# More dense blocks between shorter lists in the up stage of a two-layer encoder, with VectorE's order written out around the lists

## The chip, the core and the metric

The kernel is one program on one core of a Trainium2 chip. The core has five engines that run side by side and wait for each other by semaphores: TensorE (PE in the profile; PEld is its weight load), VectorE (DVE), ScalarE (ACT), GpSimd (POOL) and SyncE (SP). SP issues plain DMA transfers, POOL issues the indirect ones, whose rows are picked by a table of numbers. The metric is the time of one launch on the device in microseconds, as the median of some runs; smaller is better. A profile is taken of one more execution, and its span is a little shorter than that execution's time.

## The reference

Two layers over 256 frames of width 1024: first a latent attention, then a sparse attention, each followed by a channel mixer that picks experts by product keys. The mixer is what matters here:

```python
def _peer(x, w_q, sub_keys, w_down, w_up):
    ...
    best, pos = lax.top_k(cand, PEER_TOPK)
    expert = jnp.take_along_axis(cand_idx, pos, axis=-1)
    gate = jax.nn.softmax(best, axis=-1)
    ...
    def per_block(args):
        x_blk, e_blk, g_blk = args
        u = w_down[e_blk]
        a = jnp.einsum('td,ted->te', x_blk, u).astype(jnp.float32)
        hg = (jax.nn.gelu(a, approximate=False) * g_blk).astype(w_up.dtype)
        return jnp.einsum('te,ted->td', hg, w_up[e_blk]).astype(x_blk.dtype)
```

Each frame picks 8 x 16 = 128 of 16384 experts. For each it needs one row of `w_down` and one of `w_up`, both 1024 wide. All is float32.

## The kernel before

*Numbers.* Each float32 operand is cut in two float16 halves, a high one (`hi`, on ScalarE, L137) and what is left (`lo`, on VectorE, L146). A product is three matmuls on PE: hi with hi, hi with lo, lo with hi. The same holds for the second operand, cut into `xh` and `xl`. Every `lo` and `xl` also sums its entries into a column, from which the program judges at its end whether the halves and the lists were good enough; if not, the whole trunk runs once more in full float32.

*The mixer.* The 16384 experts stand as 128 blocks of 128 rows. The **down stage** takes every block against all 256 frames (`d`, 24 matmuls of 256 columns a block), applies the gelu and multiplies by the gates, which `place` spreads out from one-hot products (`G`). The result `A` (128 rows x 128 blocks x 256 frames) stays on the chip in `arena`. Beside `G` the product `seen` notes, for each half of the frames, which block's expert in a row is used by anybody.

The **up stage** sums `A` times `w_up` into four banks `y`: 12 matmuls of 512 columns for a block that both halves of the frames use, 6 for a block that only one half uses (`rows`). The first `HEAD` = 16 blocks are dense: their rows of `w_up` come by a plain DMA on SP (L192) and their `A` is taken from `arena`. For the other 112 blocks the program doesn't take all. In each of the 128 rows it makes three lists of the block numbers that are used: by both halves (`JB` = 40 places), by the first half only and by the second half only (`JO` = 24 places each). What doesn't fit goes into a common tail that is spread over all rows (`TB` = 12 places of 128 entries; a row may give up to `ROWTAIL` = 32). That makes 40 + 12 listed blocks of both halves and 48 of one. Each listed block is put together by POOL: one indirect DMA for its 128 rows of `w_up` (L190, tile `raw`) and one for its 128 rows of `A` (L1537 for both halves, L1543 for one, tiles `V` and `U`). For the second, `A` was copied to memory before (`abuf`, by `store`, L1454, in pieces of `CHUNKED` = 8 blocks and one half). Blocks are taken in groups of two or three that share one pair of slots in `xh` and `xl`.

*The lists* are made by `lists`, a generator (L1358 onward) that `list_on` moves forward step by step, partly beside the last down blocks, partly beside the dense head. It picks the eight largest numbers at a time (L1376, L1377), counts the tail, sums the counts over the rows with one small matmul (`base`, L1396), builds one-hot tiles (`wide`, `sent`, `to`) and sends the tail's entries to their rows with 32 small matmuls (`moved`, L1431). At its end stand `up_at` and `act_at`, the numbers that POOL's indirect DMAs read.

*What sets the order.* A scheduler orders each engine's instructions, except where the code links them: `pe`, `dve` and `act` put an instruction behind the one that the same chain issued last. In this kernel PE's matmuls of the two stages are linked, the lists' own are not. SP's transfers (plain rows of `w_up`, pieces of `abuf`) are one queue in order, and so are POOL's.

*The stream.* `Stream.get` hands out the next block of weights. It keeps six `raw` buffers and six pairs of `hi` and `lo`; it splits three blocks ahead and loads up to five more.

Of the kernel before, what the change touches and what calls it, by code (L numbers as in the profile page):

```python
# [10 lines left out]
F32 = mybir.dt.float32  # L11
F32R = mybir.dt.float32r
F16 = mybir.dt.float16
# [55 lines left out]
HEAD = 16  # L69
JB, JO, TB, ROWTAIL = 40, 24, 12, 32  # L70
# [3 lines left out]
CHUNKED = 8  # L74


def _up_order():
# [34 lines left out]
    return groups, items  # L112


GROUPS, ITEMS = _up_order()

# [32 lines left out]
class Stream:  # L149
# [16 lines left out]
    def listed(self, table, rows, order, unit, kind):  # L166
        for c in order:
            self.rows[len(self.blocks)] = table, rows[:, c : c + 1]
            self.blocks.append((None, D, unit))
            self.kind.append(kind)  # L170
# [129 lines left out]
def tile_trunk(ctx: ExitStack, tc: tile.TileContext, ins, out: bass.AP, short, shared):  # L300
# [56 lines left out]
    if short:  # L357
        abuf = dram.tile([(NKEYS + 1 - HEAD) * P, T], F32, tag="abuf", name="abuf")
# [8 lines left out]
        nc.vector.memset(weight16[:, :HEAD], 0.0)  # L367
        zero = arena[:, 30720 - T : 30720]
        nc.vector.memset(zero, 0.0)
        nc.sync.dma_start(abuf[(NKEYS - HEAD) * P :, :], zero)  # L370
# [764 lines left out]
    def peer(li):  # L1135
# [222 lines left out]
        def lists():  # L1358
# [7 lines left out]
            nc.vector.tensor_scalar(two, seen[:, : 2 * P].rearrange("p (t b) -> p t b", b=P), 0.0, None, op0=ALU.is_gt)  # L1366
            nc.vector.tensor_tensor(key[:, 0, :], two[:, 0, :], two[:, 1, :], op=ALU.mult)
            yield
            nc.vector.tensor_tensor(key[:, 1, :], two[:, 0, :], two[:, 1, :], op=ALU.is_gt)
            nc.vector.tensor_tensor(key[:, 2, :], two[:, 1, :], two[:, 0, :], op=ALU.is_gt)  # L1370
            nc.vector.tensor_tensor(key[:, 0:3, :], key[:, 0:3, :], weight16[:, None, :].to_broadcast([P, 3, P]),
                                    op=ALU.mult)
            yield

            def take(o, k):
                nc.vector.max(o, k)  # L1376
                nc.vector.match_replace(k, o, k, 0.0)  # L1377
# [6 lines left out]
            nc.vector.tensor_tensor(over, key[:, 0, :], key[:, 1, :], op=ALU.add)  # L1384
            nc.vector.tensor_tensor(over, over, key[:, 2, :], op=ALU.add)
# [4 lines left out]
            nc.vector.max(m8, over)  # L1390
            nc.vector.tensor_scalar(valid, more, 0.0, None, op0=ALU.is_gt)
            nc.vector.tensor_reduce(count[:, 0:1], valid, axis=AX.X, op=ALU.add)
            n16 = small.tile([P, 1], F16, tag="n16", name="n16", bufs=1)
            nc.vector.tensor_copy(n16, count[:, 0:1])
            p = ps("base")
            nc.tensor.matmul(p[:, 0:1], below16, n16, start=True, stop=True)  # L1396
            vals = small.tile([P, ROWTAIL, 2], F16, tag="vals", name="vals", bufs=1)
            nc.vector.tensor_copy(vals[:, :, 0], more)
            nc.vector.tensor_scalar(vals[:, :, 1], valid, row, None, op0=ALU.mult)
            yield  # L1400
            nc.vector.tensor_copy(count[:, 1:2], p[:, 0:1])
            rank, block = got[:, 3, 2 * ROWTAIL : 3 * ROWTAIL], got[:, 3, 3 * ROWTAIL :]
            nc.vector.tensor_scalar(rank, iota16[:, :ROWTAIL], count[:, 1:2], None, op0=ALU.add)
            nc.vector.tensor_scalar(block, rank, 1.0 / P, -(P - 1) / (2.0 * P), op0=ALU.mult, op1=ALU.add)
            nc.vector.tensor_scalar(block, block, MAGIC, None, op0=ALU.add)
            nc.vector.tensor_scalar(block, block, -MAGIC, None, op0=ALU.add)
            at16 = small.tile([P, 2, ROWTAIL], F16, tag="at16", name="at16", bufs=1)
            nc.vector.scalar_tensor_tensor(at16[:, 0, :], block, -float(P), rank, op0=ALU.mult, op1=ALU.add)
# [137 lines left out]
        def cut_group(g):  # L1546
            if g >= len(GROUPS):
                return
# [203 lines left out]
```

## Time and profile before

| what | us |
|---|---|
| median of three runs | 1775.59 (1774.29 to 1784.7) |
| the profiled execution, in all | 1780.97 |
| its span | 1778.7 |
| up stage of layer 0, first to last `y` matmul | 549.1 to 866.5 |
| up stage of layer 1 | 1450.4 to 1760.7 |
| POOL busy from 560 to 850, with 198 indirect DMAs | 228.5 |

How to read it: the page gives each engine's busy time and, in 40 slices, the tenths in which it was busy. A row of the timeline gives the start, how long, the engine, the line, the operation with its tiles (output, arrow, inputs) and in brackets how long the engine sat idle before, and for whom. A row of the windows gives, for a stretch, each engine's busy time with its number of instructions, then the clock that PE was granted (1.00 is full speed), the DMA engines' share and GB/s. A matmul of 512 columns is listed with 0.38 us, of which a part overlaps the next; its pace is read from start to start.

### The profile page before, as it was taken

What the parts mean: (1) busy time and instruction counts of PE and PEld (TensorE: products, weight loads), DVE (VectorE), ACT (ScalarE), POOL (GpSimd) and SP (SyncE); (2) the same over time, 40 slices, a digit from 0 to 9 for tenths busy, and PEclk for the clock granted to TensorE, in tenths of its full rate; (3) what the DMA queues carried; (4) which work ended last, traced back from release to release, by engine and by line L of the source; (5) the groups of instructions that cost most, each with busy time, mean ns of one, the idle gap of its engine ahead of it and who ended that gap; (6) DMA issues with size and microseconds to landing.
All of it is one profiled execution on the core that took longest, in us unless ns stands there. A gap on an engine that the chain in (4) does not pass through costs nothing.

```text
span 1778.7 us, 32888 instructions
## 1 busy us (share of the span) xinstructions
PE 1604.0 (90%) x12209; PEld 1152.1 (65%) x12209; DVE 1341.3 (75%) x3210; ACT 1060.5 (60%) x1846; POOL 636.5 (36%) x530
## 2 busy tenths in 40 slices
PE   9999999999988977877899999998999979788775
PEld 7688888899974433332478698887999944333232
DVE  8689999789997454554788799997899986445445
ACT  7666656788864444444577666666888735344343
POOL 2011343000003777777222112540000017777773
PEclk9999999899998989999999999998999989999997
DMA  9455656348578666666765455564466597666664
GB/s 343 152 171 183 197 199 218 126 159 272 184 214 293 212 222 204 221 210 218 268 230 199 169 184 201 196 209 149 160 210 237 193 325 234 210 212 226 214 198 156
DMA packets 156476, 372.44 MB, mean 209 GB/s; under 512 B 14096, under 2 KB 72592, under 8 KB 156304
## 3 DMA queue, kind: packets, MB, share of 16 engines
q1 hardware_dynamic: 119152, 244.91, 41.1%
q0 software_dynamic: 36864, 124.81, 21.8%
q8 instruction: 97, 1.59, 0.4%
q14 instruction: 75, 0.61, 0.1%
q10 hardware_dynamic: 288, 0.52, 0.1%
HBM read 336.50 MB, written 33.69 MB: 208 GB/s over the span
## 4 chain that ended last, share of the span: by engine, by line
PE 56%; POOL 13%; issue 12%; DMA 11%; DVE 6%; ACT 2%; POOLq 0%; DVEq 0%; SPq 0%; ACTq 0%
PE d L420 37%; POOL raw L190 6%; DMA raw<-in_up,up_at 4%; DMA U<-abuf,act_at 3%; PE G L420 3%; PE y L420 3%; PE q L420 2%; POOL V L1543 2%; POOL V L1537 2%; DVE lo L146 2%; DMA V<-abuf,act_at 2%; PE pq L420 2%; PE seen L420 2%; POOL U L1543 2%; PE v L420 1%
## 5 line engine op out<-in xcount | busy, mean ns | idle before, releaser
L146 DVE SCALAR_TENSOR_TENSOR lo<-raw,hi 128x1024 f16<-128x1024 f32 (+1 forms) x547 | 687.8, 1262 | 327.4 <-ACT hi L137 324.5
L137 ACT ACTIVATE hi<-raw 128x1024 f16<-128x1024 f32 (+1 forms) x547 | 570.6, 1050 | 504.8 <-DMA raw<-in_up,up_at 262.6
L420 PE MATMUL d<-xh,hi 128*128 128x256 f16 x2048 | 563.4, 275 | 0.0
L420 PE MATMUL d<-xl,hi 128*128 128x256 f16 x2048 | 563.3, 275 | 0.0
L420 PE MATMUL d<-xh,lo 128*128 128x256 f16 x2048 | 563.0, 275 | 0.0
L420 PEld LDWEIGHTS <-hi 128*128 128x128 f16 x5016 | 492.1, 99 | 61.9 <-issue 1.5
L420 PEld LDWEIGHTS <-xh 128*128 128x128 f16 x1744 | 173.0, 100 | 342.9 <-issue 165.5
L420 PE MATMUL y<-hi,xh 128*128 128x512 f16 x800 | 247.2, 390 | 61.7 <-ACT hi L137 61.4
L420 PE MATMUL y<-lo,xh 128*128 128x512 f16 x800 | 249.3, 391 | 44.3 <-DVE lo L146 43.7
L420 PEld LDWEIGHTS <-lo 128*128 128x128 f16 x2508 | 247.3, 99 | 30.6
L190 POOL DMA_INDIRECT raw<-in_up,up_at x200 | 243.2, 1216 | 61.5 <-issue 50.6
L420 PE MATMUL y<-hi,xl 128*128 128x512 f16 x800 | 246.9, 388 | 0.0
L1335 ACT ACTIVATE gate<-hot,rest 128x128 f16<-128x128 f16 x512 | 167.4, 405 | 19.4 <-DVE hot L1329 17.9
L1537 POOL DMA_INDIRECT V<-abuf,act_at x52 | 56.5, 1086 | 293.4 <-ACT hi L137 269.9
L420 PEld LDWEIGHTS <-xl 128*128 128x128 f16 x872 | 86.9, 100 | 111.0 <-issue 12.9
L227 POOL TENSOR_TENSOR lo<-raw,hi 128x1024 f16<-128x1024 f32 x26 | 59.7, 2295 | 189.8 <-ACT hi L225 169.4
L420 PE MATMUL G<-gate,hot 128*128 128x128 f16 x1024 | 99.2, 222 | 12.6 <-DVE gate L1331 12.5
L1329 DVE TENSOR_TENSOR hot<-iota,place 128x1024 f16<-128x1024 f16 x128 | 88.1, 690 | 26.8 <-PE G L420 26.0
L420 PEld LDWEIGHTS <-hot 128*128 128x128 f16 x1536 | 95.0, 114 | 13.8 <-DVE gate L1331 5.2
L1250 POOL TENSOR_TENSOR arena<-arena 128x800 f32<-128x800 f16 x32 | 72.4, 2262 | 70.7 <-DVE arena L1247 70.7
L656 POOL TENSOR_SCALAR fit<-fit 128x1 f32<-128x1 f32 x1 | 0.5, 459 | 260.3 <-ACT fit L655 260.3
L420 PE MATMUL seen<-gate,hot 128*128 128x128 f16 x512 | 91.3, 222 | 0.0
(269 smaller groups left out, 1907.6 us busy)
## 6 DMA issues: line engine op xcount, KB each, us to landing
raw<-in_down SPq DMA_DIRECT2D x256, 512.0 KB, 3.4
abuf<-arena SPq DMA_DIRECT2D x56, 512.0 KB, 6.3
raw<-in_up SPq DMA_DIRECT2D x32, 512.0 KB, 5.1
raw<-in_peer_q SPq DMA_DIRECT2D x24, 512.0 KB, 4.6
raw<-in_dsa_qk SPq DMA_DIRECT2D x16, 512.0 KB, 4.4
raw<-in_mla_w_o SPq DMA_DIRECT2D x8, 512.0 KB, 5.6
arena<-in_peer_q SPq DMA_DIRECT2D x8, 512.0 KB, 5.9
raw<-in_dsa_v SPq DMA_DIRECT2D x8, 512.0 KB, 6.3
```

Of the source, the lines that this page charges most:

```text
L137: return nc.scalar.copy(o, src) if unit == 1.0 else nc.scalar.mul(o, src, unit)
L146: return nc.vector.scalar_tensor_tensor(o, src, unit, hi, op0=ALU.mult, op1=ALU.subtract, accum_out=total)
L190: self.nc.gpsimd.indirect_dma_start(t, None, table, bass.IndirectOffsetOnAxis(ap=at, axis=0))
L227: nc.gpsimd.tensor_tensor(lo, raw, hi if short else hi.bitcast(F32), op=ALU.subtract)
L420: return pe(lambda: nc.tensor.matmul(o, l, r, start=start, stop=stop, skip_group_check=True))
L656: nc.gpsimd.tensor_scalar(fit[:, 4:5], fit[:, 4:5], LEAST, None, op0=ALU.is_ge)
L1250: nc.gpsimd.tensor_tensor(o.rearrange("p k c -> p c k"), same, cell[t][:, h, :, None].to_broadcast([P, CELLS, TOPK]), op=ALU.mult)
L1329: nc.vector.tensor_tensor(hot, iota4[:, None].to_broadcast([P, 2, P, 4]), place16[:, :, None, four].to_broadcast([P, 2, P, 4]), op=ALU.is_ ...
L1335: nc.scalar.mul(gate[:, 1, j, :], hot[:, 1, :, j], rest[:, t : t + 1])
L1537: nc.gpsimd.indirect_dma_start(t[:, 2 * slot : 2 * slot + 2, :].rearrange("p a b -> p (a b)"), None, abuf, bass.IndirectOffsetOnAxis(ap=at ...
L1543: nc.gpsimd.indirect_dma_start(t[:, 2 + h, :], None, halves, bass.IndirectOffsetOnAxis(ap=at, axis=0))
```

## The change

The first 46 blocks of the up stage are dense now (`DENSE`), in place of 16. Twenty of them are the head; the other 26 stand in pairs between the listed blocks. The lists cover the remaining 82 blocks: 24 places for both halves, 16 and 16 for one, 16 for the tail, so that 40 listed blocks of both halves and 32 of one remain, 72 in all. `_up_order` gives the pairs their places, `_up_plan` numbers the pairs of slots for dense and listed blocks together, and one loop walks through all 118 uses. `A` goes to memory from block 46 on, in pieces of four blocks.

```diff
-HEAD = 16
-JB, JO, TB, ROWTAIL = 40, 24, 12, 32
+DENSE, HEAD = 46, 20
+JB, JO, TB, ROWTAIL = 24, 16, 16, 32
...
-CHUNKED = 8
+CHUNKED = 4
...
-    return groups, items
+    behind = {}
+    pairs = list(range(HEAD, DENSE, 2))
+    for n, k in enumerate(pairs):
+        behind.setdefault((LISTED - 10) * (n + 1) // len(pairs), []).extend((None, j, (0, 1), None) for j in (k, k + 1))
+    order = []
+    for i, x in enumerate(items):
+        order.append(x)
+        order += behind.get(i, [])
+    assert len(order) == LISTED + DENSE - HEAD
+    return groups, order
...
-        ws.listed(up_rows, up_at, [c for _, _, _, c in ITEMS], UP_UNIT, "most")
+        for g, slot, _, c in ITEMS:
+            if g is None:
+                ws.add(ins["up"][li][slot : slot + 1], unit=UP_UNIT, kind="most")
+            else:
+                ws.listed(up_rows, up_at, c, UP_UNIT, "most")
```

In `lists` every instruction of VectorE goes through `dve` and every matmul through `pe`, so that they are linked with the splits and the stages' matmuls. `base` gets a step of its own, and each group of eight `moved` matmuls is issued one step after its `to` tile:

```diff
             def take(o, k):
-                nc.vector.max(o, k)
-                nc.vector.match_replace(k, o, k, 0.0)
+                dve(lambda: nc.vector.max(o, k))
+                dve(lambda: nc.vector.match_replace(k, o, k, 0.0))
...
+            yield
             p = ps("base")
-            nc.tensor.matmul(p[:, 0:1], below16, n16, start=True, stop=True)
...
+            pe(lambda: nc.tensor.matmul(p[:, 0:1], below16, n16, start=True, stop=True))
             yield
...
+            def send():
+                j0, to = sends.pop(0)
+                for j in range(8):
+                    w = sent[:, j0 + j].rearrange("p v n -> p (v n)")
+                    pe(lambda: nc.tensor.matmul(p[:, : 2 * TB], to[:, j, :], w, start=j0 + j == 0,
+                                                stop=j0 + j == ROWTAIL - 1, skip_group_check=True))
+
             for j0 in range(0, ROWTAIL, 8):
                 to = ohp.tile([P, 8, P], F16, tag="V", name="to")
-                nc.vector.tensor_tensor(to, iota16[:, None, :].to_broadcast([P, 8, P]),
-                                        at16[:, 0, j0 : j0 + 8, None].to_broadcast([P, 8, P]), op=ALU.is_equal)
-                for j in range(8):
-                    nc.tensor.matmul(p[:, : 2 * TB], to[:, j, :], sent[:, j0 + j].rearrange("p v n -> p (v n)"),
-                                     start=j0 + j == 0, stop=j0 + j == ROWTAIL - 1, skip_group_check=True)
+                dve(lambda: nc.vector.tensor_tensor(to, iota16[:, None, :].to_broadcast([P, 8, P]),
+                                                    at16[:, 0, j0 : j0 + 8, None].to_broadcast([P, 8, P]), op=ALU.is_equal))
+                sends.append((j0, to))
                 yield
...
+                send()
...
                 if groups == 64:
-                    listing[0] = listing[0] or lists()
-                    list_on(8)
+                    if listing[0] is None:
+                        chains["dve"] = None
+                        listing[0] = lists()
+                    list_on(3)
...
         if short:
...
+            cut(0)
+            for i, (n, slot, tiles) in enumerate(USES):
+                if i == FIRSTS[n]:
+                    cut(n + 1)
+                    if PAIRS[n][0] == "listed":
+                        gather(PAIRS[n][1] + 3)
+                if i < len(USES) - STAGGER:
+                    rows(y4, made[n][slot], ws.get(), i == 0, False, tiles)
+                if i < HEAD - 9:
+                    list_on(1)
+                if i == HEAD - 9:
+                    list_on(99)
+                    chains.pop("dve")
+                    chains.pop("pe")
+                if i < HEAD - 3:
+                    store(0, NKEYS)
+                    store(1, NKEYS)
+                if i == HEAD - 4:
+                    assert stored == [NKEYS, NKEYS], stored
+                    for g in range(3):
+                        gather(g)
```

PE at the end of layer 0's down stage, before: `base` and the first `moved` follow a product of one of the last down blocks (`d_7427`), with two more down blocks behind them.

```order
L420 LDWEIGHTS lo_7346
L420 MATMUL d_7427<-xh,lo_7346 128x256
L1396 LDWEIGHTS below_121
L1396 MATMUL base<-n_7495,below_121 128x1
L1431 LDWEIGHTS to
L1431 MATMUL moved<-sent,to 128x24
```

PE at `base` in the changed kernel: it follows the third block of the up stage (`hi_7513` and `lo_7514` are that block's halves, `hi_7564` is the fourth's).

```order
L452 LDWEIGHTS xl
L452 MATMUL y_7559<-hi_7513,xl 128x512
L1433 LDWEIGHTS below_121
L1433 MATMUL base<-n_7607,below_121 128x1
L452 LDWEIGHTS xh
L452 MATMUL y_7556<-hi_7564,xh 128x512
```

`base` went from the down stage into the head of the up stage, and the eight `moved` matmuls that followed it at once now stand after the 8th, 9th, 10th and 11th up block, eight each.

VectorE at the one-hot tiles of the lists, before: they stand in one run ahead of the next split (`lo_7660` is the fifth up block's).

```order
L1409 CAST at_7507<-U 128x32
L1419 TENSOR_TENSOR wide_7512<-iota_105,at_7507 128x384
L1428 TENSOR_TENSOR to<-iota_105,at_7507 128x1024
L1422 TENSOR_TENSOR sent<-wide_7512,vals 128x32x12 x2
L1428 TENSOR_TENSOR to<-iota_105,at_7507 128x1024 x3
L146 SCALAR_TENSOR_TENSOR lo_7660,sums<-raw_7432,hi_7659 128x1024
L146 SCALAR_TENSOR_TENSOR xl,sums<-arena,xh 128x512 x3
L1434 COPY keys<-moved 128x12
```

The same place in the changed kernel (`lo_7691` is the ninth up block's).

```order
L1454 TENSOR_TENSOR wide_7685<-iota_105,at_7659 128x512
L1457 TENSOR_TENSOR sent<-wide_7685,vals 128x32x16
L175 SCALAR_TENSOR_TENSOR lo_7691,sums<-raw_7568,hi_7690 128x1024
L1457 TENSOR_TENSOR sent<-wide_7685,vals 128x32x16
L175 SCALAR_TENSOR_TENSOR xl,sums<-arena,xh 128x512
L175 SCALAR_TENSOR_TENSOR lo_7713,sums<-raw_7590,hi_7712 128x1024
L1472 TENSOR_TENSOR to<-iota_105,at_7659 128x1024
L175 SCALAR_TENSOR_TENSOR lo_7735,sums<-raw_7619,hi_7734 128x1024
```

One or two splits stand between two steps of the lists now, and the one-hot tiles come about four blocks later.

POOL from its last product of the expert choice to its first indirect DMAs of layer 0, before (`raw_7801` is the first listed block's).

```order
L1250 TENSOR_TENSOR arena<-arena 128x50x16 x8
L1537 DMA V<-abuf,act_at 128x256
L1543 DMA V<-abuf,act_at 128x128 x2
L1537 DMA U<-abuf,act_at 128x256 x2
L1537 DMA V<-abuf,act_at 128x256 x2
L1537 DMA U<-abuf,act_at 128x256
L1543 DMA U<-abuf,act_at 128x128 x2
L190 DMA raw_7801<-in_up,up_at 128x1024
```

And in the changed kernel (`raw_7884` is the first listed block's, `raw_8027` the sixth's).

```order
L1282 TENSOR_TENSOR arena<-arena 128x50x16 x8
L218 DMA raw_7884<-in_up,up_at 128x1024
L218 DMA raw_7903<-in_up,up_at 128x1024
L218 DMA raw_7923<-in_up,up_at 128x1024
L1587 DMA V<-abuf,act_at 128x256
L1593 DMA V<-abuf,act_at 128x128 x2
L1587 DMA U<-abuf,act_at 128x256 x2
L1587 DMA V<-abuf,act_at 128x256 x2
L1587 DMA U<-abuf,act_at 128x256 x2
L218 DMA raw_7941<-in_up,up_at 128x1024
L218 DMA raw_7961<-in_up,up_at 128x1024
L1587 DMA V<-abuf,act_at 128x256
```

Three rows of `w_up` now come ahead of the first gathers of `A`; from there the two kinds alternate as before, 144 in a layer in place of 200.

More of the change, by code (lines that the diff above doesn't have):

```diff
@@ L111, in _up_order, with _up_plan @@
     assert len(items) == LISTED and len({x[3] for x in items}) == LISTED
-    return groups, items
-GROUPS, ITEMS = _up_order()
+    behind = {}
[8 more added lines that the diff above has]
+    return groups, order
+GROUPS, ITEMS = _up_order()
+def _up_plan():
+    pairs, uses, firsts, at = [], [], [], {}
+    head = [(None, k, (0, 1), None) for k in range(HEAD)]
+    for i, (g, slot, tiles, _) in enumerate(head + ITEMS):
+        key = ("dense", slot // 2 * 2) if g is None else ("listed", g)
+        if key not in at:
+            at[key] = len(pairs)
+            pairs.append(key)
+            firsts.append(i)
+        uses.append((at[key], slot % 2 if g is None else slot, tiles))
+    for n in range(len(pairs) - 4):
+        assert max(i for i, u in enumerate(uses) if u[0] == n) < firsts[n + 3], n
+    return pairs, uses, firsts
+PAIRS, USES, FIRSTS = _up_plan()
 class Split:
@@ L164, in __init__, with listed @@
         self.rows = {}
[L166 to L170, printed above, removed]
+    def listed(self, table, rows, c, unit, kind):
+        self.rows[len(self.blocks)] = table, rows[:, c : c + 1]
+        self.blocks.append((None, D, unit))
+        self.kind.append(kind)
     def add(self, src, w=D, unit=W_UNIT, kind="both"):
@@ L1395, in lists @@
+            vals = small.tile([P, ROWTAIL, 2], F16, tag="vals", name="vals", bufs=1)
+            dve(lambda: nc.vector.tensor_copy(vals[:, :, 0], more))
+            dve(lambda: nc.vector.tensor_scalar(vals[:, :, 1], valid, row, None, op0=ALU.mult))
+            yield
             p = ps("base")
-            nc.tensor.matmul(p[:, 0:1], below16, n16, start=True, stop=True)
-            vals = small.tile([P, ROWTAIL, 2], F16, tag="vals", name="vals", bufs=1)
-            nc.vector.tensor_copy(vals[:, :, 0], more)
@@ L1551, in cut_group @@
             hh, al = xh[:, slot, :], xl[:, slot, :]
             total = split.total("most")
-            split.high(hh, a, A_UNIT)
-            split.low(al, a, A_UNIT, hh, total)
-            made[g] = [(hh[:, j, :], al[:, j, :]) for j in range(2)]
+            act(lambda: split.high(hh, a, A_UNIT))
+            dve(lambda: split.low(al, a, A_UNIT, hh, total))
+            made[n] = [(hh[:, j, :], al[:, j, :]) for j in range(2)]
         if short:
-            for k in range(HEAD):
-                rows(y4, operand(k), ws.get(), k == 0, False)
-                if k < HEAD - 8:
-                    list_on(4 if k < 3 else 3)
+            cut(0)
@@ L1580, in peer @@
+                if i == len(USES) // 2:
                     middle_loads()
-            items = [(made[g][slot], tiles) for g, slot, tiles, _ in ITEMS[-STAGGER:]]
+            items = [(made[n][slot], tiles) for n, slot, tiles in USES[-STAGGER:]]
         else:
```

136 lines of the change are left out of this document (66 added, 70 removed).

## The prediction

> **What bounds the kernel now.** I read the page's engine shares and slices first, then the timeline of the two places that the change touches (the end of the down stage and the up stage, once in each layer), then the up stage by windows, and last the durations of single steps.
>
> ```profile
> span 1778.7 us, 32888 instructions
> PE 1604.0 (90%) x12209; PEld 1152.1 (65%) x12209; DVE 1341.3 (75%) x3210; ACT 1060.5 (60%) x1846; POOL 636.5 (36%) x530
> ...
> PE   9999999999988977877899999998999979788775
> ...
> POOL 2011343000003777777222112540000017777773
> ```
>
> PE is full almost everywhere except where POOL's row shows sevens: the two listed parts of the up stage. Its edges on PE, by the timeline, with a stretch of matmuls without a gap:
>
> ```profile
> 549.13 0.59 PE L420 MATMUL y<-hi,xh 128*128 128x512 f16 x2
> ...
> 851.64 0.59 PE L420 MATMUL y<-hi,xh 128*128 128x512 f16 x2
> ...
> 858.55 0.59 PE L420 MATMUL y<-lo,xh 128*128 128x512 f16 x2
> ...
> 866.09 0.38 PE L420 MATMUL y<-hi,xl 128*128 128x512 f16 x1
> ...
> 1450.38 0.59 PE L420 MATMUL y<-hi,xh 128*128 128x512 f16 x2
> ...
> 1760.33 0.38 PE L420 MATMUL y<-hi,xl 128*128 128x512 f16 x1
> ```
>
> So the up stage runs 317.3 us in layer 0 and 310.4 us in layer 1. From 851.64 to 858.55 stand 32 matmuls, 0.216 us each; a block of both halves (12 matmuls) is 2.59 us, one of a single half (6) is 1.30 us. Before, a layer has 16 + 52 blocks of both halves and 48 of one: 1104 matmuls, 238 us. The other 70 to 80 us are waits, and the windows say whose:
>
> ```profile
> core 0: us, PE busy (x) PEld busy (x) DVE busy (x) ACT busy (x) POOL busy (x), PEclk, DMA share, GB/s
> 560.00:850.00 290.00, 236.19 (x982) 98.58 (x981) 147.32 (x281) 125.80 (x141) 228.53 (x198) 0.95 0.68 219
> 1460.00:1745.00 285.00, 233.04 (x989) 98.20 (x987) 149.92 (x287) 127.20 (x142) 223.89 (x198) 0.96 0.69 224
> 549.00:600.00 51.00, 51.00 (x245) 23.22 (x244) 30.79 (x69) 25.43 (x31) 31.16 (x26) 1.00 0.77 255
> 1460.00:1470.00 10.00, 10.00 (x48) 4.51 (x46) 5.98 (x13) 5.27 (x6) 7.09 (x7) 1.00 0.91 343
> 1490.00:1500.00 10.00, 10.00 (x48) 4.51 (x46) 7.39 (x14) 5.64 (x7) 7.56 (x9) 1.00 0.59 178
> 1740.00:1760.00 20.00, 20.00 (x94) 9.03 (x93) 12.92 (x24) 10.38 (x13) 8.19 (x8) 1.00 0.58 201
> ...
> ACT hi L137 <- DMA raw<-in_up,up_at: 141.4, 70, 4.2
> POOL raw L190 <- issue: 23.5, 77, 0.3
> ```
>
> POOL issues 198 indirect DMAs in 290 us, 1.46 us a step (1.44 in layer 1), and between two of them lie only 0.3 us: it never waits for anybody. ScalarE's `hi` waits 141 us of layer 0's up stage for the listed rows. DMA moves 219 GB/s there and 343 GB/s elsewhere, so it has room. And the last row is the counter-proof: once POOL has issued nearly all, PE is full on the same listed blocks. **POOL's steps bound the up stage.**
>
> The second loss stands just before it:
>
> ```profile
> 503.86 5.24 PE d L420 x48
> ...
> 536.60 0.16 PE L1396 MATMUL base<-n,below 128*128 128x1 f16 x1 [9.11 <-DVE n L1394]
> 540.95 0.39 PE L1431 MATMUL moved<-sent,to 128*128 128x24 f16 x8 [4.18 <-DVE sent L1422]
> 541.34 4.62 PE d L420 x23
> 546.35 2.74 PE d L420 x25
> ...
> 1437.70 0.16 PE L1396 MATMUL base<-n,below 128*128 128x1 f16 x1 [9.11 <-DVE n L1394]
> 1442.05 0.39 PE L1431 MATMUL moved<-sent,to 128*128 128x24 f16 x8 [4.19 <-DVE sent L1422]
> ```
>
> `base` and `moved` sit in PE's queue ahead of the last 48 down matmuls, and VectorE is not there yet. PE stops at 536.60 - 9.11 = 527.49 and begins the up stage at 549.13, 21.6 us for 48 matmuls that take 5.24 us elsewhere: 16.4 us lost (the first 23 at half pace). Layer 1 has the same two waits.
>
> **The change, part by part.** All of it is worked against the profiled execution: span 1778.7 us, 1781.0 us with what lies around it; the three timed runs have a median of 1775.6 us, to which the sum is then applied.
>
> *PE's work.* 46 + 40 blocks of both halves and 32 of one are 1032 + 192 = 1224 matmuls a layer: 264.3 us, 26 us more than before. This is the up stage's floor if nothing else binds.
>
> *POOL's work.* 72 listed rows and 16 x 3 + 12 x 2 = 72 gathers replace 100 and 100: 144 steps in place of 200. At 1.46 us that is 210 us, under PE's 264 us. What a step will cost is the unknown:
>
> ```profile
> 716.16 1.22 DVE L146 SCALAR_TENSOR_TENSOR lo<-raw,hi 128x1024 f16<-128x1024 f32 x1
> ...
> 716.74 1.47 POOL L1537 DMA_INDIRECT V<-abuf,act_at  x1 [0.30 <-issue]
> 718.51 0.95 POOL L1543 DMA_INDIRECT V<-abuf,act_at  x1 [0.30 <-issue]
> ```
>
> A step that begins while VectorE is inside `lo` is longer by about what is left of `lo` (716.74 to 717.3, then 0.9); one that begins on its own takes 0.95, 1.25 with the gap. VectorE is busy 51% of 560 to 850; the same work squeezed into some 215 us makes it about 70%, so the 0.21 us that a step loses on average may grow to 0.29: 1.54 us. Against that, from 1490 to 1500 VectorE was busy 74% and POOL still issued 9 steps in 10 us. Ends 1.25 and 1.55; I take 1.5, beside the 1.46 measured over 198 steps.
>
> [...]
>
> *Where POOL can still hold PE.* The lists are ready about 38 us after the first `y` matmul (below). From there a block's row is ready after its place in POOL's order times the step, 5.3 us to land, 1.05 for `hi`, 1.23 for `lo`, less 0.43 in which PE can use `hi` alone:
>
> ```profile
> raw<-in_up,up_at POOLq DMA_INDIRECT x200, 5.3
> ...
> L137 ACT ACTIVATE hi<-raw 128x1024 f16<-128x1024 f32 (+1 forms) x547 | 570.6, 1050 | 504.8 <-DMA raw<-in_up,up_at 262.6
> ...
> L146 DVE SCALAR_TENSOR_TENSOR lo<-raw,hi 128x1024 f16<-128x1024 f32 x100 | 122.8, 1228 | 140.7 <-ACT hi L137 140.4
> L146 DVE SCALAR_TENSOR_TENSOR xl<-U,xh 128x512 f16<-128x512 f32 x19 | 13.1, 691 | 0.5 <-ACT xh L137 0.5
> ```
>
> Walked through block by block, the tightest place is block 45: its row is POOL's 50th step, ready at 38 + 49 s + 7.2; PE, without waits, is there after 4.0 + 39 x 2.59 + 6 x 1.30 + 0.6 = 113.4. The wait is 49 s - 68.2: 3 us at 1.46, 5.3 at 1.5, 7.8 at 1.55. Behind it PE has 156 us of matmuls left and POOL 94 steps, 141 us; the 26 dense blocks between the listed ones are what gives POOL that time. Only above 1.56 does a late place bind instead (block 106, 135th step: 134 s - 200.4). I take 5.3 us a layer.
>
> *The lists' work.* VectorE's rows of it, and of what precedes the first `xl`:
>
> ```profile
> L1478 ACT ACTIVATE d<-d x66: 183/411/580, 323.0 to 1451.1; 128x512 f32<-128x512 f32 x6, 128x24 f32<-128x24 f32 x2, 128x48 f32<-128x48 f32 x2, 128x64 f32<-128x64 f32 x2
> ...
> 530.80 0.59 DVE arena L1479
> ...
> 533.05 0.31 DVE U L1376
> 533.38 0.36 DVE V L1377 x2
> ...
> 537.73 0.19 DVE U L1406
> ...
> L1428 DVE TENSOR_TENSOR to<-iota,at 128x1024 f16<-128x1024 f16 x4 | 4.8, 1222 | 2.9 <-PE moved L1431 2.9
> ...
> L1422 DVE TENSOR_TENSOR sent<-wide,vals 128x384 f16<-128x384 f16 x2 | 1.0, 552 | 0.0
> ```
>
> It no longer stands in front of PE: `base` comes after the third up block, `moved` after the 8th to 11th, about 1.0 us of PE in all. VectorE now does it between the splits of the dense head. There each two blocks take PE 5.18 us and VectorE two `lo` and one `xl`, 3.15 us, which leaves 2.0 us a pair, 14 us over seven pairs. The lists' rest there is four `to` (4.9), `wide` and two `sent` (2.2, a third longer than now), one pick of eight (0.7) and some twenty small ones of 0.2: about 12 us. It fits, just, and `up_at` is written when VectorE is at block 16, about 4.5 + 14 lo x 1.2 + 7 xl x 0.65 + 12 = 38 us after the first `y`. The price is at the very start: the first `xl` stands behind the last product of gate and activation, two sums and three picks. That is 0.6 (ScalarE's gelu) + 0.6 + 0.6 + 3 x 0.67 + 0.7 = 4.5 us after the last down matmul, of which PE covers 0.9 with `hi` and `lo`: a wait of about 4 us, bounded by 0 and by the 16.4 us of before.
>
> *Stores.* 82 blocks in place of 112 go to memory, in 42 transfers of half the size a layer instead of 28. They end while PE is in the dense head and nothing reads them before step 4 of POOL's order; SP's dense rows are queued behind them as before, and the head ran without a gap (549 to 600: PE 51 of 51 us). I cost them at nothing; if a dense row came late, a `hi` would wait a landing, some 5 us.
>
> *Sum.* The up stage becomes 4.0 + 264.3 + 1.0 + 5.3 = 274.6 us. Layer 0: 317.3 - 274.6 + 16.4 = 59.1. Layer 1: 310.4 - 274.6 + 16.4 = 52.2. Together 111 us: span 1667, and 1775.6 - 111 = **1664 us**.
>
> **The rivals.**
> 1. *POOL stays the bound.* For it: the lock shown above and a denser VectorE. Against: the row from 1490 to 1500. At a step of 1.65 the late place gives a wait of 20.7 in place of 5.3 us a layer: 1695 us; from 1.6 to 1.75 it is 1682 to 1722.
> 2. *VectorE is late through the head*, since slack (14) and work (12) lie close; PE then waits there about as long as it did before the up stage: 2 x 12.4 us back, 1689 us. Against: `lo` runs three blocks ahead of PE.
> 3. *Slower.* The same lock, but each step held for most of a `lo`. All of the gain is gone when 134 s - 200.4 reaches 61 us, a step of 1.95 us; the longest steps now are that long, the mean is far from it. At 2.1 us it would be about 1815 us.
> 4. *The shorter lists don't hold.* Then the whole trunk runs again in full precision, above 3400 us. Counted from the reference's own choices, the common tail would take 1832 and 1879 entries of 2048 in the two layers, and at most 23 of 32 in a row, so it should hold.
>
> **How the numbers follow.** The forecast as worked (step 1.25 to 1.58, first wait 1 to 6 us) gives 1648 to 1682 us and has 0.62; rival 1 has 0.23, rival 2 0.09, rivals 3 and 4 0.03 each. The range 1648 to 1712 leaves out the top of rival 1, rivals 3 and 4 and a little below: about 0.16. A change of 1% is what a measurement of this kernel tells from none. Faster by more: 0.62 + 0.23 + 0.09 = 0.94; rival 3 lies about the old time, 0.02 within and 0.01 above; slower in all 0.04.
>
> **What would show it.** Right: PE in nines through both up stages, 1224 matmuls in about 275 us; `base` without 9 us before it; POOL with real gaps (waits for VectorE's `lo`, not only 0.3 us) in the second half of the stage. Wrong: POOL's steps at 1.6 us or more with 0.3 us between them; PE waiting for `xl` or `lo` through the dense head; a second trunk in the trace.

## The result, and the profile after

The changed kernel takes 1674.1 us (median of four runs, 1673.4 to 1676.4) where the kernel before took 1774.9 in the same group: a ratio of 0.942, 95% interval 0.939 to 0.946. The forecast was 1664.

The head of the page and five of its rows of slices, for the profiled execution of the changed kernel (1676.4 us in all):

```profile
span 1674.6 us, 33334 instructions
...
PE 1606.8 (96%) x12449; PEld 1164.4 (70%) x12449; DVE 1349.2 (81%) x3212; ACT 1064.7 (64%) x1863; POOL 527.6 (32%) x419
...
PE   9999999899998999999999999998999989999995
...
DVE  8689999788998757676788799998889988566665
...
POOL 2011255000000278877032012441000000788772
PEclk9999999999999999999999999999999999999998
```

PE, 90% busy before, is 96% busy, with nines (and some eights) where it had sevens and eights beside POOL's work. POOL's row still shows sevens and eights there: it has fewer steps, but is hardly less dense. The timeline of PE's first `y` matmuls and of two later ones in layer 1, the waits of PE in each up stage, and a window over the listed part of layer 0 (the lines of the code have shifted: L452 is the matmul, L175 `lo` and `xl`, L166 `hi` and `xh`, L218 a listed `raw`, L1587 and L1593 the gathers, L1433 `base`):

```profile
533.21 0.60 PE L452 MATMUL y<-hi,xh 128*128 128x512 f16 x2 [1.07 <-ACT xh L166]
539.90 1.03 PE L452 MATMUL y<-hi,xl 128*128 128x512 f16 x2 [5.66 <-DVE xl L175]
...
1475.44 0.59 PE L452 MATMUL y<-hi,xh 128*128 128x512 f16 x2 [0.78 <-ACT hi L166]
...
1630.51 0.59 PE L452 MATMUL y<-hi,xh 128*128 128x512 f16 x2 [0.52 <-ACT hi L166]
```

```profile
PE y L452 <- DVE xl L175: 5.4, 1, 5.4
PE y L452 <- DVE lo L175: 2.9, 5, 0.7
PE y L452 <- ACT hi L166: 2.0, 3, 0.8
PE y L452 <- ACT xh L166: 1.3, 1, 1.3
```

```profile
576.00:800.00 224.00, 222.55 (x1032) 100.70 (x1031) 142.09 (x278) 120.21 (x140) 172.26 (x142) 1.00 0.80 267
```

(The second fence is layer 1; in layer 0 it is 5.7 for `xl`, 1.1 for `xh`, and 1.5 for listed rows.) The up stage now runs from 533.21 to 807.27 in layer 0 and from 1377.49 to 1657.40 in layer 1:

| us | before | forecast | after |
|---|---|---|---|
| first `y` of layer 0 | 549.1 | 16.4 earlier | 533.2, 15.9 earlier |
| up stage, layer 0 | 317.3 | 274.6 | 274.1 |
| from there to the first `y` of layer 1 | 583.9 | 16.4 less | 570.2, 13.7 less |
| up stage, layer 1 | 310.3 | 274.6 | 279.9 |

The span is 7.6 us above the 1667 of the forecast, and all of that lies behind layer 0's up stage. The table looks like a forecast that came true term by term. The experiments say that the split into terms was wrong all the same.

### The profile page after: what moved, and what is told of

Same layout as the page of the kernel before. It is cut to its first block, busy times and chain, and to the rows that moved or that the text cites. A ratio compares the mean times of both kernels' runs of the same rounds, so it can differ in the third digit from the quotient of the medians.

```text
span 1674.6 us, 33334 instructions
## 1 busy us (share of the span) xinstructions
PE 1606.8 (96%) x12449; PEld 1164.4 (70%) x12449; DVE 1349.2 (81%) x3212; ACT 1064.7 (64%) x1863; POOL 527.6 (32%) x419
## 4 chain that ended last, share of the span: by engine, by line
PE 51%; issue 13%; DVE 11%; DMA 11%; POOL 10%; ACT 3%; SPq 0%; POOLq 0%; DVEq 0%; ACTq 0%
PE d L452 34%; DMA raw<-in_up,up_at 6%; PE y L452 5%; POOL raw L218 5%; DVE lo L175 5%; PE G L452 3%; PE pq L452 2%; PE seen L452 2%; ACT hi L166 2%; POOL V L1593 1%; POOL U L1587 1%; POOL V L1587 1%; DMA U<-abuf,act_at 1%; POOL U L1593 1%; PE qw L452 1%
## 5 line engine op out<-in xcount | busy, mean ns | idle before, releaser
L175 DVE SCALAR_TENSOR_TENSOR lo<-raw,hi 128x1024 f16<-128x1024 f32 (+2 forms) x550 | 696.8, 1277 | 207.5 <-ACT hi L166 203.4
L166 ACT ACTIVATE hi<-raw 128x1024 f16<-128x1024 f32 (+2 forms) x550 | 570.0, 1049 | 374.9 <-DMA raw<-in_up,up_at 166.9
L452 PE MATMUL d<-xh,lo 128*128 128x256 f16 x2048 | 559.3, 273 | 1.6 <-DVE lo L175 1.6
L452 PE MATMUL d<-xh,hi 128*128 128x256 f16 x2048 | 559.5, 273 | 0.0
L452 PE MATMUL d<-xl,hi 128*128 128x256 f16 x2048 | 559.3, 273 | 0.0
L452 PEld LDWEIGHTS <-hi 128*128 128x128 f16 x5016 | 489.3, 98 | 59.0 <-issue 1.5
L218 POOL DMA_INDIRECT raw<-in_up,up_at x144 | 182.5, 1268 | 612.1 <-DMA raw<-in_up 561.8
L452 PEld LDWEIGHTS <-xh 128*128 128x128 f16 x1904 | 185.4, 98 | 232.0 <-issue 12.9
L452 PE MATMUL y<-hi,xl 128*128 128x512 f16 x880 | 265.4, 381 | 11.1 <-DVE xl L175 11.1
L452 PE MATMUL y<-hi,xh 128*128 128x512 f16 x880 | 265.6, 381 | 5.2 <-ACT hi L166 2.8
L452 PE MATMUL y<-lo,xh 128*128 128x512 f16 x880 | 265.8, 381 | 3.6 <-DVE lo L175 3.6
L452 PEld LDWEIGHTS <-lo 128*128 128x128 f16 x2508 | 245.9, 98 | 33.1 <-DVE lo L175 3.6
L1367 ACT ACTIVATE gate<-hot,rest 128x128 f16<-128x128 f16 x512 | 167.3, 406 | 22.3 <-DVE hot L1361 20.7
L452 PEld LDWEIGHTS <-xl 128*128 128x128 f16 x952 | 93.0, 98 | 125.2 <-DVE xl L175 13.8
L452 PE MATMUL G<-gate,hot 128*128 128x128 f16 x1024 | 98.2, 221 | 15.7 <-DVE gate L1363 15.7
L452 PEld LDWEIGHTS <-hot 128*128 128x128 f16 x1536 | 93.8, 114 | 17.6 <-DVE gate L1363 7.0
L452 PE MATMUL seen<-gate,hot 128*128 128x128 f16 x512 | 90.3, 220 | 0.0
L251 ACT ACTIVATE raw<-raw 128x1024 f32<-128x1024 f32 x27 | 28.5, 1056 | 93.1 <-DMA raw<-in_down 82.1
L1363 DVE TENSOR_TENSOR gate<-hot,gate 128x512 f16<-128x512 f16 x128 | 87.3, 682 | 0.0
```

Of the source, the lines that this page charges most:

```text
L166: return nc.scalar.copy(o, src) if unit == 1.0 else nc.scalar.mul(o, src, unit)
L175: return nc.vector.scalar_tensor_tensor(o, src, unit, hi, op0=ALU.mult, op1=ALU.subtract, accum_out=total)
L218: self.nc.gpsimd.indirect_dma_start(t, None, table, bass.IndirectOffsetOnAxis(ap=at, axis=0))
L251: self.act(lambda: nc.scalar.mul(raw, raw, unit))
L452: return pe(lambda: nc.tensor.matmul(o, l, r, start=start, stop=stop, skip_group_check=True))
L1363: engine.tensor_tensor(gate[:, 0], hot[:, 1].rearrange("p c j -> p j c"), gate16[:, four, None].to_broadcast([P, 4, P]), op=ALU.mult)
```

## The experiments

The kernel before was run beside each group. It took 1804, 1783 and 1785 us there (1775 in the runs above), so times are compared inside a group, or as ratios to it.

| kernel | us | ratio to before, 95% | up stage, layers 0 and 1 | POOL's first step, layer 0 |
|---|---|---|---|---|
| group 1: `all_front` | 1772.2 | 0.983 (0.980 to 0.986) | 325.3, 320.2 | 572.8 |
| `order_only` | 1835.9 | 1.018 (1.015 to 1.021) | 364.2, 363.6 | 578.5 |
| `no_order` | 1677.9 | 0.931 (0.928 to 0.934) | 277.0, 278.9 | 564.3 |
| `dense56` | 1688.7 | 0.935 (0.931 to 0.939) | 287.7, 288.9 | 571.6 |
| group 2: `after_b` (the change) | 1675.1 | 0.940 (0.935 to 0.945) | 275.9, 277.3 | 573.0 |
| `old_pace` | 1667.3 | 0.935 (0.930 to 0.939) | 264.3, 264.3 | 552.4 |
| `both` | 1679.3 | 0.940 (0.935 to 0.945) | 277.9, 278.3 | 577.2 |
| `dense50` | 1668.1 | 0.935 (0.930 to 0.940) | 273.5, 279.6 | 571.9 |
| group 3: `after_c` (the change) | 1679.4 | 0.941 (0.938 to 0.944) | 274.2, 277.5 | 574.1 |
| `no_order_b` | 1662.0 | 0.930 (0.928 to 0.933) | 274.2, 272.9 | 563.3 |
| `pace5` | 1663.6 | 0.932 (0.930 to 0.935) | 264.9, 265.1 | 552.8 |
| `dense50_pace5` | 1661.9 | 0.932 (0.930 to 0.934) | 264.9, 265.1 | 550.6 |

In the kernel before, POOL's first step of layer 0 is at 560.9.

Group 1 needs a caution. In its four traces, and in none of the others, PE has stretches in which it waits between single matmuls, and the profile puts these waits down to `issue`, that is, to nothing it shows: 32.6 us in all in `all_front`, 72.7 in `order_only`, 11.4 in `no_order` and 12.1 in `dense56`. The kernel before was slower there too (1804 us), but has no trace in that group. What causes these stretches is open; the stages of group 1 in the table contain them.

**All dense blocks in front.** Is it the number of steps, or the dense blocks between the listed ones?

```diff
-DENSE, HEAD = 46, 20
+DENSE, HEAD = 46, 46
```

(The lists, the stores and the first gathers stay at the blocks where they were.)

> The same 46 dense blocks and the same 144 steps of POOL, but all 46 dense blocks stand ahead of the 72 listed ones; the lists are made at the same place. Theory (it is the 26 dense blocks between the listed ones that give POOL time): a listed row's tile comes free only when PE is some eight blocks ahead of it, so POOL begins about 36 blocks after the first y matmul, at about 6 + 36 x 2.59 = 99 us, and 144 steps of 1.45 to 1.55 and some 8 us of landing and cutting bring the last block to 316 to 330 us: the up stage is 40 to 55 us longer a layer and the time 1755 to 1785 us, with PE waiting for hi of the listed rows as before the change. Rival (the smaller number of steps alone was enough): 1674 us within 5.

It took 1772 us, with both stages in the span expected (325 and 320; 20.7 and 11.9 us of them are PE's waits for `issue`). The ratio, 0.983, would be 1745 beside 1775; either way it is far from the rival's 1674. POOL in layer 0:

```profile
572.82 1.24 POOL L1587 DMA_INDIRECT V<-abuf,act_at  x1 [282.17 <-DMA raw<-in_up]
...
633.94 0.94 POOL L218 DMA_INDIRECT raw<-in_up,up_at  x1 [48.58 <-DMA raw<-in_up]
636.62 0.94 POOL L218 DMA_INDIRECT raw<-in_up,up_at  x1 [1.73 <-DVE lo L175]
```

The lists are ready at the same time, but after its first gathers POOL sits idle for 48.6 us, because the tiles for listed rows come free only as PE moves on through the dense ones. The next rows wait for VectorE's `lo` in the same way. From 645.54 on its steps, 1.54 us each on average (1.49 in layer 1), set the pace, and the stage ends some 12 us after the last of them, as it did before the change. Fewer steps alone were not enough: dense blocks have to stand beside them.

**The order by hand alone, on the old sizes.**

```diff
-DENSE, HEAD = 46, 20
-JB, JO, TB, ROWTAIL = 24, 16, 16, 32
+DENSE, HEAD = 16, 16
+JB, JO, TB, ROWTAIL = 40, 24, 12, 32
...
-CHUNKED = 4
+CHUNKED = 8
...
-                    list_on(3)
+                    list_on(4)
```

> VectorE's order by hand and base and moved among the up stage's matmuls, with the old sizes (16 dense blocks in front, 100 listed ones, 200 steps, stores of eight blocks). Theory A (the two parts of the prediction add up): the first y comes 14 to 16 us earlier in each layer and the time falls by as much, 1744 us within 6. Theory B (POOL's steps set the end, and they start when the lists are ready, not when y starts): the lists are ready at about the time at which they were before (554 us in layer 0), POOL starts within a few us of 561 us, and what the earlier y wins is waited for at the listed rows: 1765 to 1780 us.

It is 1.8% slower than before. Theory A (the parts add up) falls; theory B had the right mechanism and too small a price. POOL's first step, of the kernel before and then of this one:

```profile
560.93 2.27 POOL L1537 DMA_INDIRECT V<-abuf,act_at  x1 [269.93 <-ACT hi L137]
```

```profile
578.48 1.24 POOL L218 DMA_INDIRECT raw<-in_up,up_at  x1 [285.49 <-DVE act_at L1488]
```

The first `y` came at 534.8, 14 us earlier than before, but `act_at`, spread thinly between the splits of the head, is written later, and POOL begins 17.5 us later. In layer 1, counted from the end of layer 0's stage, it begins 15.8 us later. With 200 steps to go POOL sets the end, and these 33 us are as much as the medians differ by (32). What PE waits for the lists at the end of the down stage was not a pure loss; it bought an early start for POOL.

The profiled execution, the slowest of the five, shows more than that: its stage of layer 0 ends 32.5 us later. The steps themselves are no longer (1.14 us on average, 1.16 before), but six pauses of POOL, 22.8 us in all, stand between them (0.8 us before), and PE has 30.7 us of the waits that the profile names no cause for. The end of the longest such stretch, the longest pause of POOL right behind it, and PE's sum for the stage:

```profile
623.94 0.59 PE L452 MATMUL y<-hi,xl 128*128 128x512 f16 x1 [2.20 <-issue]
...
628.65 1.68 POOL L218 DMA_INDIRECT raw<-in_up,up_at  x1 [6.23 <-DVE lo L175]
...
PE y L452 <- issue: 30.7, 26, 3.2
```

**The new sizes without the order by hand.** The lists' instructions are not linked any more, nor are PE's matmuls and VectorE's splits in the head; the lists are still taken up in three portions after each pair of down blocks.

```diff
             seen = begun.pop("seen")
+            dve = pe = lambda emit: emit()
...
-                        chains["dve"] = None
                         listing[0] = lists()
```

> The new sizes without the order by hand: the lists' instructions on VectorE and TensorE stand where the scheduler puts them. Theory (with the new sizes PE is the bound, so each us of a late first y is a us of the time): base and moved stand ahead of down matmuls again, or VectorE is late elsewhere in the head, 10 to 16 us a layer: 1692 to 1708 us. Rival (with the smaller lists the scheduler's order costs little): 1674 us within 5.

> The new sizes without the order by hand, at the new rate of three portions, beside the changed kernel on the same chip (its first run stood in a group without the changed kernel). Theory (the order by hand wins nothing with these sizes: without it PE has no wait at the first xl, but meets the listed rows earlier by as much and waits there): within 5 us of the changed kernel. Rival (the order by hand is worth what the prediction gave it, 12 to 16 us a layer): 25 us or more above it.

The theory of the first run (10 to 16 us lost a layer) falls. The second run fits neither its theory (within 5 us of the changed kernel) nor its rival (25 us or more above it): it is 17 us *below* the changed kernel by the medians (ratios 0.930 and 0.941, whose intervals don't meet), of which its profiled execution shows 6.5. The first run had no run of the changed kernel beside it, and its stages contain 5.4 and 6.0 us of the waits for `issue`, which the second run doesn't have. Without the links `base` stays among the up matmuls, PE goes from `d` to `y` without a pause and never waits for the first `xl`, and POOL begins 10.7 us earlier than in `after_c` (563.3 and 574.1). PE pays part of that back at the first listed blocks:

```profile
527.59 0.27 PE L452 MATMUL d<-xh,lo 128*128 128x256 f16 x1
527.69 0.59 PE L452 MATMUL y<-hi,xh 128*128 128x512 f16 x2
...
603.98 0.59 PE L452 MATMUL y<-hi,xh 128*128 128x512 f16 x2 [1.08 <-ACT hi L166]
...
622.10 0.59 PE L452 MATMUL y<-hi,xh 128*128 128x512 f16 x2 [1.58 <-ACT hi L166]
```

So it isn't the order by hand that took the 9 us in front of `base` away. It is the slower rate (three portions in place of eight), which writes `base` behind the down stage.

**The old rate.** As the last, with eight portions: `base` and `moved` stand ahead of down matmuls again, as before the change. (`base` keeps its own step, and each group of `moved` its place one step after its `to`.)

```diff
-                    list_on(3)
+                    list_on(8)
```

> The new sizes without the order by hand, and with the lists' work taken up in the down stage at the old rate (eight portions after each pair of blocks in place of three), so that base is written ahead of the last down matmuls again. Theory (the 16 us that the change won at the end of the down stage come from where base and moved stand, not from VectorE's order by hand, which the kernel without that order already did without): 9 and 4 us before base and moved are back, y starts 12 to 16 us later in each layer, but the lists are ready earlier too, so nothing is waited for at the listed rows: 20 to 32 us slower than the changed kernel. Rival (with the smaller lists VectorE is in time wherever base stands): within 5 us of the changed kernel.

The wait in front of `base` is back, 9.5 us, with 96 down matmuls behind it in place of 48; the 4.2 us in front of `moved` are not. Theory and rival both missed: the kernel is 8 us *faster* than the changed one (1667.3 and 1675.1; each of its four runs is below each of the other's, though the intervals of the ratios overlap). PE in layer 0:

```profile
528.88 0.16 PE L1434 MATMUL base<-n,below 128*128 128x1 f16 x1 [9.52 <-DVE n L1428]
...
536.19 0.35 PE L1468 MATMUL moved<-sent,to 128*128 128x32 f16 x8
...
542.24 0.59 PE L452 MATMUL y<-hi,xh 128*128 128x512 f16 x2
```

POOL's first step there, and its waits for `lo` in the stage:

```profile
552.36 1.27 POOL L1586 DMA_INDIRECT V<-abuf,act_at  x1 [261.95 <-DMA arena<-x]
...
POOL raw L218 <- DVE lo L175: 30.4, 22, 4.6
```

`y` begins 10.3 us later than in `after_b`, but POOL begins 20.7 us earlier, and the up stage takes 264.3 us in both layers: 1224 matmuls of 0.2159 us, without one wait. POOL now has the gaps that the prediction named as the sign of a POOL with time in hand: 30.4 us in which it waits for `lo` to free a tile, against 4.3 in the changed kernel. In that one, PE's early start runs into `xl`, then `hi` and `lo` of listed rows, and the stage is 10 to 16 us longer for it.

**The first wait.** Two edits at once: the first `xl` ahead of the last three portions, and the stores of the second half in the up stage's head. Nothing is left out.

```diff
-                    list_on(3)
-                    store(1, b0)
-                    store(1, b0)
+                    if b0 < NKEYS - 2:
+                        list_on(3)
...
             cut(0)
+            list_on(3)
...
                     store(1, NKEYS)
+                    store(1, NKEYS)
```

> Two edits at the first y matmuls: the first xl of the up stage is put ahead of the last three portions of the lists, and the stores of the second half of the rows are issued in the up stage's head, not in front of the dense rows at the end of the down stage. Theory A (the first wait of 5.4 to 5.7 us is lost time): it falls to 1 or 2 us, and the time by 7 to 9 us. Theory B (the wait only shifts: the lists are ready no earlier, so PE meets the listed rows that much too early): the first wait falls too, but PE waits 3 to 5 us for hi about block 20 to 45, and the time is within 3 us of the changed kernel.

Theory B. The wait for `xl` falls from 5.7 to 3.0 us, POOL begins 4.2 us later, and PE meets the listed rows too early:

```profile
537.82 0.61 PE L452 MATMUL y<-hi,xl 128*128 128x512 f16 x1 [2.98 <-DVE xl L175]
...
632.85 0.59 PE L452 MATMUL y<-hi,xh 128*128 128x512 f16 x2 [1.82 <-ACT hi L166]
```

The stage is 277.9 us in place of 275.9, the time 1679 in place of 1675: no gain.

**Doses.** Fewer steps of POOL at the same work of PE, and more work of PE:

```diff
-DENSE, HEAD = 46, 20
-JB, JO, TB, ROWTAIL = 24, 16, 16, 32
+DENSE, HEAD = 50, 20
+JB, JO, TB, ROWTAIL = 24, 16, 12, 32
```

> 50 dense blocks, a common tail of 12 blocks in place of 46 and 16: the same 1224 matmuls, but 68 listed blocks and 136 steps of POOL in place of 72 and 144. Theory (PE bounds the up stage now): only the waits for listed rows, 1.5 and 4.9 us, can go, so 0 to 6 us less than the changed kernel. Rival (POOL still bounds it): 8 steps of 1.55 us a layer, 25 us less.

1668.1 beside 1675.1: 7 us less, just outside the theory's 0 to 6, where 16 steps in all, at 1.55, would be 25. POOL's number of steps no longer sets the pace. The two up stages of the profiled executions come to 553.1 us here and 553.2 in `after_b`, so the traces don't show the 7 us there; the run-to-run spread (4 us here, 9 in `after_b`) does not allow more.

```diff
-DENSE, HEAD = 46, 20
-JB, JO, TB, ROWTAIL = 24, 16, 16, 32
+DENSE, HEAD = 56, 20
+JB, JO, TB, ROWTAIL = 16, 16, 16, 32
```

> 56 dense blocks (36 between listed ones), lists of 16 + 16 + 2 x 16: 64 listed blocks, 128 steps, 1248 matmuls in place of 1224 a layer. Theory (PE bounds the up stage, POOL has just enough time): 24 matmuls of 0.216 us more, 5.2 us a layer, less at most the 1.5 and 4.9 us that PE waits for listed rows: 1680 to 1685 us. Rival (POOL still bounds it, 16 steps fewer are 24 us fewer): below 1665 us.

By its own us it is near the theory (1680 to 1685) and far from the rival (below 1665); by its ratio, in a group in which the kernel before took 1804, it would be 1659 beside 1775. So it decides nothing between the two. Only ratios, 0.935 and 0.940 or so, set it against the changed kernel, and they overlap.

Against `no_order`, which stood in the same group, it is 10.8 us slower in the median and its stages are 10.7 and 10.0 us longer. The 24 matmuls more a layer cost 5.2 us of that. Most of the rest is at the first `xl`, which `no_order` doesn't wait for: 5.7 us. (In `after_b` the ten `y` matmuls behind this wait took 0.42 us each, in place of 0.22.) Both kernels also have one of group 1's stretches near the first listed blocks. Here it is:

```profile
585.74 0.95 POOL L218 DMA_INDIRECT raw<-in_up,up_at  x1 [0.30 <-issue]
...
591.75 0.38 PE L452 MATMUL y<-lo,xh 128*128 128x512 f16 x1 [0.19 <-issue]
593.88 0.38 PE L452 MATMUL y<-lo,xh 128*128 128x512 f16 x1 [1.75 <-issue]
...
590.00:600.00 10.00, 4.99 (x17) 1.45 (x15) 3.17 (x6) 2.11 (x2) 7.87 (x8) 0.85 0.59 194
```

The scheduler put ten gathers ahead of the first listed `raw` here (in the changed kernel three `raw` go first), so that row is issued 14.1 us after POOL starts. But that isn't what PE waits for: by the count of its matmuls these waits stand in the last two dense blocks of the head, before the first listed one.

**Early lists and a shorter wait.** Five portions after each pair of down blocks, with 46 and with 50 dense blocks, no order by hand:

```diff
-                    list_on(3)
+                    list_on(5)
```

> The new sizes without the order by hand, five portions of the lists after each pair of down blocks: base stands about 50 matmuls later than at eight portions, still ahead of the first y. Theory (what counts is that the lists are ready early, against what PE waits before base for them): the wait before base falls from 9.5 to 3 to 6 us and the lists come 0 to 4 us later than at eight, so the up stage stays at 264 to 268 us: 3 to 10 us below the kernel with eight portions, about 15 us below the changed kernel, 1657 to 1665 us. Rival (the wait before base only moves): the same as with eight portions, 8 us below the changed kernel.

> As before (five portions, no order by hand), with 50 dense blocks and a common tail of 12: the same 1224 matmuls, 136 steps of POOL in place of 144. Theory (with early lists PE never waits for a listed row, so POOL's steps are worth nothing): within 3 us of the kernel with 46 dense blocks and five portions. Rival (at five portions the lists are late enough for POOL to hold PE): 3 to 10 us less than that kernel.

```profile
533.26 0.16 PE L1434 MATMUL base<-n,below 128*128 128x1 f16 x1 [6.92 <-DVE n L1428]
...
541.05 0.59 PE L452 MATMUL y<-hi,xh 128*128 128x512 f16 x2
```

`pace5` is 1663.6 us, as its theory had it, and 16 below the changed kernel, with intervals that don't meet. The wait before `base` is 6.9 us (3 to 6 were expected), and the stage stays at 265. Whether it is faster than with eight portions is not shown: `old_pace` stood in another group, and the ratios, 0.932 and 0.935, overlap. With 50 dense blocks it is 1661.9, the same within the spread: eight steps fewer a layer are worth nothing once PE never waits for a listed row. These two and `no_order_b` (1662.0) beat both given kernels, by some 7% and 1%.

## Why the prediction was right, and where it was not

*What bounds the kernel: right.* POOL's steps held the old up stage. `all_front` and `order_only` bring that bound back, and `dense50` and `dense50_pace5` show that the number of POOL's steps no longer is the bound. One sign of being right did not come: in the changed kernel POOL waits for `lo` for only 4.3 us in layer 0, and steps to within 14 us of the stage's end. It has little time in hand.

*PE's floor of 264.3 us: right.* `old_pace` runs both stages in exactly that.

*POOL's step: 1.5 taken, 1.54 and 1.58 measured* in the two layers (573.33 to 793.19 and 1418.44 to 1643.91, first to last of 144). The two other traces of the changed kernel have 1.49 to 1.56. VectorE is busy 142 of 224 us there, 63% and not 70%. The prediction's estimate of 1.54, worked out from the 0.21 us that a step lost on average, was the better one, though for a busier VectorE. A step that begins inside a `lo` or an `xl` takes 1.39 us on average, any other 0.94; 0.42 us of the `lo` or `xl` are left there, about what the step is longer by. (Before, it is 1.31 and 0.95, with 0.50 left.) This much of the lock that rivals 1 and 3 speak of is in the traces. The other way round there is none: 161 `lo` begin while a step is running, and take 1.22 us, as long as the 1.23 of the others, so a step that started first did not hold VectorE to its end. In the kernel before, inside the step that the prediction shows at 718.51:

```profile
719.06 1.23 DVE L146 SCALAR_TENSOR_TENSOR lo<-raw,hi 128x1024 f16<-128x1024 f32 x1 [1.67 <-ACT hi L137]
```

*The hold at block 45: there is one, but not quite there, and not 5.3 us.* Counted by PE's matmuls and numbered from 0, the waits stand at block 36, in layer 1 also at 42 and 43, and at 104 and 105, the late place. They come to 1.5 us in layer 0 and 4.9 in layer 1. POOL's first 25 steps took 1.41 us each in layer 0, and PE came later than the 4.0 us of the sum allowed.

*The first wait: too small.* 4.0 was forecast; 5.7 and 5.4 for `xl`, and 1.1 to 1.3 for `xh` ahead of it, were measured. The stores costed "at nothing" are part of it, by the mechanism named there: eight of them, 5.96 us, stood in front of a dense row, its `hi` waited 4.25 us, and VectorE, bound by its order, sat idle behind it before the last picks and the first `xl`:

```profile
517.88 5.96 SPq L1500 DMA_DIRECT2D abuf<-arena  x8
523.94 0.80 SPq L220 DMA_DIRECT2D raw<-in_up  x1
```

```profile
529.51 1.06 ACT L166 ACTIVATE hi<-raw 128x1024 f16<-128x1024 f32 x1 [4.25 <-PE d L452]
```

```profile
531.08 0.69 DVE L1525 TENSOR_TENSOR arena<-arena,d 128x512 f32<-128x512 f32 x1 [3.05 <-ACT d L1524]
539.15 0.68 DVE L175 SCALAR_TENSOR_TENSOR xl<-arena,xh 128x512 f16<-128x512 f32 x1
```

The row names PE's `d`, but the transfer issued at 523.94 landed 5.5 us later, at 529.4, just ahead of this `hi`. In `after_b`, the same kernel, the row names the transfer itself:

```profile
528.29 1.06 ACT L166 ACTIVATE hi<-raw 128x1024 f16<-128x1024 f32 x1 [4.57 <-DMA raw<-in_up]
```

How much of the first wait the stores are was not run by itself: `both` moved them, together with another edit, and got 2.7 us of the wait back, without a gain in time.

*The step that failed: the 16.4 us a layer for the reordering, added to the gain of the sizes.* The prediction took PE's pause before `base` for time that a later `base` would save, less 4 us. Its ledger had 12.4 us a layer, 25 in all, for the new place of the lists' work, and 86 for the sizes (317.3 and 310.4 less 270.6 each). Measured beside each other, the sizes with the old rate (`old_pace`) bring 116 us, and going from there to the changed kernel *costs* 8. The comparison is not quite clean, since `old_pace` no longer waits in front of `moved` and its first `y` come 6.9 and 1.3 us earlier than before; but 99 of the 109 us between the profiled spans are its shorter up stages. On the old sizes the order by hand was 32 us slower in group 1. So the change's gain is that of its sizes. That the total came out near is luck: two errors of some 30 us each, by the medians, had opposite signs.

The reordering has two parts, and the last group tells them apart. The slower rate alone is worth nothing: without links, three portions (`no_order_b`, 1662.0) and five (`pace5`, 1663.6) take the same time within the spread. With three the first `y` of layer 0 comes 13.4 us earlier and POOL's first step 10.5 us later. A pause before `base` and a wait at the listed rows are two ends of one thing, the time at which the lists are ready: PE starts earlier at the price of later lists, and meets them later in the stage. That was rival 2's idea (PE would wait about as long as before). The links, the order by hand itself, are the part that costs: `no_order_b` and `after_c` differ in them alone, and with them the first `y` comes 5.2 us later, POOL's first step 10.7 us later, and the time is 17 us longer by the medians.

*Open.* Why the changed kernel is 17 us above `no_order_b` in the medians when the profiled pair differs by 6.5 was not settled; its runs spread from 1671.6 to 1681.8 in that group, its profiled one is near the lowest and that of `no_order_b` is its highest, and one trace each does not show what the others do. `no_order` and the changed kernel differ in VectorE's order everywhere around the lists, so no single instruction is named as the cost of the order by hand. What slows PE in the stretches of group 1 is not known either.

## What to carry to other kernels

When two engines share a stage, a pause of the one may be what the other's head start is made of. Before counting a pause as gain, ask when the thing waited for will be ready afterwards: here a first matmul 10 us earlier came with a POOL that began 21 us later, and the stage grew by as much as was won or more. An order written by hand has to be run beside the scheduler's own; here the scheduler's was the better one. And a change in several parts needs each part run alone: the total agreed with the sum, and one of its two large terms had the wrong sign.

## What the runs showed of the hardware

Behind some pauses of PE its next matmuls ran slower for some us. In `old_pace`, behind 9.5 us in front of `base`, PE takes a `d` matmul each 0.21 us, and each 0.11 from 533.25 on, 4.4 us later; the granted clock of the ten us from 530 on is 0.84:

```profile
528.90 0.38 PE L452 MATMUL d<-xh,hi 128*128 128x256 f16 x1
529.07 0.42 PE L452 MATMUL d<-xl,hi 128*128 128x256 f16 x1
...
533.25 0.27 PE L452 MATMUL d<-xh,hi 128*128 128x256 f16 x1
533.36 0.27 PE L452 MATMUL d<-xl,hi 128*128 128x256 f16 x1
...
530.00:540.00 10.00, 10.00 (x96) 8.42 (x95) 9.30 (x13) 3.29 (x4) 0.00 (x0) 0.84 1.08 330
```

In the changed kernel (`after_c`) the ten us after the wait for the first `xl` hold 39 matmuls where 48 fit, at a clock of 0.78:

```profile
540.00:550.00 10.00, 10.00 (x39) 4.16 (x38) 7.57 (x26) 4.39 (x5) 0.00 (x0) 0.78 1.07 369
```

So that wait cost about 2 us more than it lasted (an estimate: 9 matmuls of 0.216 us). The prediction left that out of its first wait. In the changed kernel's trace of the section on the result, behind 5.66 us, 42 matmuls stand in these ten us, at a clock of 0.87. The pace right behind the wait was about half there: 0.40 us a matmul, in place of 0.216, from 539.90 to 542.71, 2.8 us; in `after_b`, behind 5.67 us, it was 0.42 from 538.68 to 542.92, 4.2 us. Shorter pauses had it behind them too: in `after_b`, in layer 1, PE waits 1.31 and 0.68 us at the first held block, around 1477, and right behind that the clock is half again (0.52 over these 3.5 us):

```profile
1478.50:1482.00 3.50, 3.50 (x10) 1.24 (x9) 3.11 (x7) 3.36 (x4) 2.66 (x3) 0.52 0.57 180
```

But not each time: in the trace of the section on the result PE waits 0.78 and 0.68 us at the same place, and the clock from 1475 to 1485 is 1.00.
